# Column sums of an 8192 x 8192 float32 matrix: three pieces of TensorE work moved within the tail of a load-bound kernel

## The chip, the cores and the metric

The kernel runs on one core of one Trainium2 chip. The time is the device time of one execution in microseconds (us). A run of a kernel gives several executions, each with its span (first to last instruction) and the mean granted TensorE clock; one execution, the first of a run, also leaves a profile (the profile of the kernel before is of an execution of 627.52 us, apart from the three in its table).

## The reference

```python
def setup_inputs():
    return {"x": np.random.randn(8192, 8192).astype(np.float32)}

def reference(x):
    return np.sum(x, axis=0)
```

The sum runs over rows. On the chip rows lie on partitions, so most of the sum is elementwise addition of row blocks by VectorE, and the last step, over the 128 partitions, is a matmul with a matrix of ones.

## The kernel before

The 8192 rows come as 32 loads of 256 rows (128 partitions x 2 rows x 8192 columns, 8 MB each) into three buffers. VectorE adds 31 of them into a running row. The last load is cut so that little work is left when its last byte has come: its first row of each partition comes in two halves of 4096 columns, its second row in six strips.

```python
STRIPS = [2048, 2048, 2048, 1024, 768, 256]
...
for h in range(2):                       # first row, two halves
    i = nc.sync.dma_start(out=rows(last, 0, c0, w), in_=xl[0][:, c0 : c0 + w])
    ...
    i.then_inc(s_half[h], 16)
for n, w in enumerate(STRIPS):           # second row, six strips
    nc.sync.dma_start(
        out=rows(last, 1, c0, w), in_=xl[1][:, c0 : c0 + w]
    ).then_inc(s_strip[n], 16)
```

For each strip n (0 to 5; "the third strip" is strip 2, "the sixth" strip 5) TensorE adds up three pieces in PSUM, the memory that it writes its sums to: **half n**, the first row's columns; **carry n**, VectorE's running row; **strip n**, the second row's columns. A piece is four matmuls on four column tiles, each recorded as two passes with a weight load apiece: 8 matmul records and 8 weight loads, 16 instructions. There are 18 pieces, 288 instructions.

```python
def half(n, sem=None):
    piece_sums(rows(last, 0), n, True, sem, 16)
def carry_sums(n):
    piece_sums(rows(near, 1), n, False, s_dve, carry[min(n, 3)])
def strip_sums(n):
    piece_sums(rows(last, 1), n, False, s_strip[n], 16).then_inc(s_pe, 1)

half(0, s_half[0]); half(1); carry_sums(0); carry_sums(1)   # one line each in the kernel
half(2, s_half[1]); strip_sums(0); strip_sums(1)
carry_sums(2)
for n in (3, 4, 5):
    half(n)
strip_sums(2); carry_sums(3); strip_sums(3)
carry_sums(4); carry_sums(5); strip_sums(4); strip_sums(5)
```

After each strip's sum, ScalarE or VectorE copies it out of PSUM, and three small stores end the program.

## Time and profile before

| | before |
|---|---|
| median of its first three executions | 627.25 us (627.19 to 627.32) |
| span of the profiled one | 625.6 us |
| bytes read | 268.44 MB, at 429 GB/s over the span |
| VectorE busy | 85% |
| TensorE busy | 2%, all after 607.5 us |
| second strip lands | 617.22 us |
| last TensorE pass | 622.51 us |

How to read it: the loads fill the span and the engines follow them. What TensorE does matters only from where it stops waiting for data. The prediction below shows the lines.

### The profile page before, as it was taken

Reading aid. Unit: us, or ns where it says so; the run is one execution under the profiler, and the core shown is the slowest. Engines: PE = TensorE matmul, PEld = TensorE weight load, DVE = VectorE, ACT = ScalarE, POOL = GpSimd, SP = SyncE. Lnnn points to the kernel's source line nnn. Section 1 sums busy time; section 2 is a strip of 40 time slices with the busy share of each in tenths; the row PEclk is TensorE's granted clock in tenths of the full one; section 3 lists DMA queues with packets and bytes.
Section 4 is the critical chain, followed back from the end, with each engine's and each line's share of the span. In section 5 each row is a group of like instructions: output and inputs, shape, how many; then the busy total and the mean of one; then the engine's idle time right before and its main releaser. Section 6 shows DMA issues by size and latency. Waiting matters only on the chain. (4 is left out here: it accounts for less than half of the span.)

```text
span 625.6 us, 571 instructions
## 1 busy us (share of the span) xinstructions
PE 13.2 (2%) x144; PEld 4.1 (1%) x144; DVE 531.2 (85%) x66; ACT 3.4 (1%) x5; POOL 0.3 (0%) x5
## 2 busy tenths in 40 slices
PE   0000000000000000000000000000000000000016
PEld 0000000000000000000000000000000000000002
DVE  0538988889888899888898888988889888899887
ACT  0000000000000000000000000000000000000001
POOL 0000000000000000000000000000000000000000
PEclk9999999999999999999999999999999999999999
DMA  9999999999999999999999999999999999999997
GB/s 402 402 469 402 465 406 465 406 465 406 448 423 432 440 419 453 402 469 402 469 402 469 402 469 402 465 406 465 406 465 406 453 419 432 440 423 448 402 435 306
DMA packets 5661, 268.49 MB, mean 429 GB/s; under 512 B 652, under 2 KB 784, under 8 KB 1052
## 3 DMA queue, kind: packets, MB, share of 16 engines
q1 hardware_dynamic: 5660, 268.47, 99.2%
q8 instruction: 1, 0.02, 0.0%
HBM read 268.44 MB, written 0.03 MB: 429 GB/s over the span
## 5 line engine op out<-in xcount | busy, mean ns | idle before, releaser
L121 DVE TENSOR_TENSOR buf<-buf,buf 128x8192 f32<-128x8192 f32 x29 | 252.1, 8693 | 58.1 <-DVEq L116 58.1
L126 DVE TENSOR_TENSOR buf<-buf 128x8192 f32<-128x8192 f32 x29 | 252.1, 8693 | 6.9 <-DVEq L116 6.9
L132 DVE TENSOR_TENSOR buf<-buf 128x8192 f32<-128x8192 f32 x1 | 8.7, 8691 | 23.1 <-DVEq L116 23.1
L94 PE MATMUL ps<-buf,ones 128*32 128x512 f32 (+3 forms) x144 | 13.2, 513 | 609.5 <-DMA buf<-in_x_dram 609.1
L81 DVE TENSOR_TENSOR buf<-buf,buf 128x4096 f32<-128x4096 f32 x2 | 8.8, 4422 | 1.6 <-DMA buf<-in_x_dram 1.6
L81 DVE TENSOR_TENSOR buf<-buf 128x2048 f32<-128x2048 f32 (+1 forms) x3 | 8.9, 3000 | 0.1
L94 PEld LDWEIGHTS ps<-buf,ones 128*32 128x32 f32 x144 | 4.1, 117 | 618.5 <-DMA buf<-in_x_dram 610.9
L217 ACT COPY res<-ps 128x512 f32<-128x512 f32 (+1 forms) x4 | 2.1, 520 | 618.7 <-PE ps L94 618.7
L217 DVE COPY res<-ps 128x256 f32<-128x256 f32 (+1 forms) x2 | 0.7, 325 | 2.0 <-PE ps L94 2.0
L217 ACT ACT_TABLE_LOAD x1 | 1.3, 1283 | 1.0 <-DVEq L106 1.0
L107 POOL MEMSET ones<- 128x32 f32 x1 | 0.1, 126 | 0.6 <-DVEq L106 0.6
L262 POOL MEMSET const-bfloat16-1.0<- 128x1 bf16 x1 | 0.1, 102 | 0.0
L262 POOL MEMSET const-uint8-127<- 128x1 uint8 x1 | 0.1, 102 | 0.0
L262 POOL MEMSET const-float32-0.0<- 128x1 f32 x1 | 0.1, 99 | 0.2 <-issue 0.2
L262 POOL MEMSET const-float32-1.0<- 128x1 f32 x1 | 0.1, 99 | 0.0
## 6 DMA issues: line engine op xcount, KB each, us to landing
buf<-in_x_dram SPq DMA_DIRECT2D x2, 2048.0 KB, 17.5
buf<-in_x_dram SPq DMA_DIRECT2D x3, 1024.0 KB, 23.6
buf<-in_x_dram SPq DMA_DIRECT2D x1, 512.0 KB, 26.4
buf<-in_x_dram SPq DMA_DIRECT2D x31, 29.7
buf<-in_x_dram SPq DMA_DIRECT2D x1, 384.0 KB, 26.8
buf<-in_x_dram SPq DMA_DIRECT2D x1, 128.0 KB, 26.7
out_dram<-res SPq DMA_DIRECT2D x2, 4.0 KB
out_dram<-res SPq DMA_DIRECT2D x1, 24.0 KB
```

What stands on the lines that cost most here:

```text
L81: i = nc.vector.tensor_tensor(out=o, in0=a, in1=b, op=ADD)
L94: i = nc.tensor.matmul(out=ps[n][32 * j : 32 * j + 32, 0 : w // NJ], lhsT=ones[:], rhs=runs[:, j], start=start, stop=True, skip_group_chec ...
L107: nc.gpsimd.memset(ones[:], 1.0).then_inc(s_one, 1)
L121: nc.vector.tensor_tensor(out=r0, in0=r0, in1=bufs[(b - 1) % NBUF][:, 1, :], op=ADD).then_inc(s_op, 1)
L126: nc.vector.tensor_tensor(out=r1, in0=r1, in1=r0, op=ADD).then_inc(s_buf[(b + 1) % NBUF], 1)
L132: nc.vector.tensor_tensor(out=rows(0, 1), in0=rows(0, 1), in1=rows(0, 0), op=ADD).then_inc(s_buf[1], 1)
L217: c = nc.vector.tensor_copy(out=o, in_=p) if n in (3, 5) else nc.scalar.copy(o, p)
L262: nc = _bacc.Bacc("TRN2", target_bir_lowering=False, num_devices=1)
```

## The change

The intent is to use a gap. TensorE stands idle for 1.39 us ahead of the second strip, while halves 3, 4 and 5, whose data is there, are done later, when TensorE is pressed. The change puts half 3 into that gap, halves 4 and 5 behind the second strip, and carry 2, which waits for VectorE's third piece, just ahead of the third strip.

```diff
         strip_sums(0)
+        half(3)
         strip_sums(1)
+        half(4)
+        half(5)
         carry_sums(2)
-        for n in (3, 4, 5):
-            half(n)
         strip_sums(2)
```

No load, no addition and no buffer is touched.

## The prediction

> **What bounds the kernel now.** The page comes first: the whole program is a stream of DMA loads, and TensorE works only at its very end.
>
> ```profile
> PE 13.2 (2%) x144; PEld 4.1 (1%) x144; DVE 531.2 (85%) x66; ACT 3.4 (1%) x5; POOL 0.3 (0%) x5
> ...
> HBM read 268.44 MB, written 0.03 MB: 429 GB/s over the span
> ```
>
> 268.44 MB in 625.6 us is the bound, with the one DMA queue at 99.2% of its 16 engines. The change does not touch a load, a VectorE addition or a buffer release; it moves eight-matmul pieces within TensorE's program. So only the tail after the last VectorE release of a buffer can move, and I read that next: the chain that ended last, in order of time (start, us, what).
>
> ```profile
> 593.61 23.61 DMA buf<-in_x_dram
> 617.22 0.04 issue
> 617.26 5.53 PE ps L94 x96
> 622.80 0.02 issue
> 622.82 0.22 DVE res L217
> ```
>
> The second strip lands at 593.61 + 23.61 = 617.22 us, then TensorE runs 96 matmuls until 622.8, and the last copy follows. 96 is twelve pieces of 8 (four column tiles, each as two float32 passes): strip 1, carry 2, halves 3, 4 and 5, strip 2, carry 3, strip 3, carries 4 and 5, strips 4 and 5. Taken alone the chain says "TensorE is the end", and a piece taken out is gained in full. Whether that holds depends on when the later strips land, which the chain does not show. So I went through the timeline in short windows. First TensorE around the second strip, with its weight loads:
>
> ```profile
> 614.81 1.06 PE L94 MATMUL ps<-buf,ones 128*32 128x512 f32 x8 [0.20 <-DMA buf<-in_x_dram]
> 617.26 0.64 PE L94 MATMUL ps<-buf,ones 128*32 128x512 f32 x4 [1.39 <-DMA buf<-in_x_dram]
> 618.22 0.13 PEld L94 LDWEIGHTS ps<-buf,ones 128*32 128x32 f32 x4 [0.80 <-DVE buf L81]
> 619.11 0.13 PEld L94 LDWEIGHTS ps<-buf,ones 128*32 128x32 f32 x4 [0.30 <-issue]
> 619.97 1.04 PE L94 MATMUL ps<-buf,ones 128*32 128x512 f32 x8
> 622.51 0.24 PE L94 MATMUL ps<-buf,ones 128*32 128x64 f32 x4
> ```
>
> TensorE is idle for 1.39 us before the second strip. Carry 2 starts at 618.22, when VectorE's third piece is there; half 3 starts at 619.11, strip 2 at 619.97 with no wait noted, and the last pass at 622.51. From 618.22 on it runs without a gap.
>
> Then the landings, for the issues of the third strip and of the last three (start of the issue from the timeline, time to landing from the list of DMA issues):
>
> ```profile
> 594.08 0.43 SPq L178 DMA_DIRECT2D buf<-in_x_dram  x1
> buf<-in_x_dram SPq DMA_DIRECT2D x1, 1024.0 KB, 25.6
> ...
> 595.03 0.43 SPq L178 DMA_DIRECT2D buf<-in_x_dram  x1
> buf<-in_x_dram SPq DMA_DIRECT2D x1, 512.0 KB, 26.4
> buf<-in_x_dram SPq DMA_DIRECT2D x1, 384.0 KB, 26.8
> buf<-in_x_dram SPq DMA_DIRECT2D x1, 128.0 KB, 26.7
> ```
>
> The six strip issues are 0.475 us apart (593.13, 593.61, 594.08, 594.56, 595.03, 595.51). Strip 2 therefore lands at 594.08 + 25.6 = 619.7, strip 3 at 594.56 + 26.4 = 621.0, strip 4 at 595.03 + 26.8 = 621.8 and strip 5 at 595.51 + 26.7 = 622.2, each to about 0.05 because the view rounds to tenths. Strip 2's matmuls at 619.97 are thus only some 0.25 us later than its data. That is the point of this case.
>
> **What the Trainium skill says.** "TensorE: Matmul & The Clock Gate", Part 3, says matmuls start and end strictly in program order and column tiles run concurrently. The trace agrees: four 512-column matmuls share one 0.43 us pass (start to start), so a piece moved in the program moves on the engine by just that. Its Part 1 says an idle window of about 3.4 us halves the array's clock. The first two halves do show 0.85 us per pass in place of 0.43 us, but the idle time to be filled is 1.39 us and the passes after it are already fast, so I count nothing for warmth. "PSUM — Partial Sum Buffer", the four PSUM rules, warns that two open accumulation groups in one bank and quadrant clear each other's bits; here each strip has its own 2 KiB tile, so the new interleaving is safe. "DMA: Bandwidth & Descriptors", section Where 436 GB/s comes from, puts the load ceiling at 435.2 GB/s; 429 measured over the span agrees, and nothing is to be had there.
>
> **The change part by part.** Durations are start-to-start spacings of the passes in the timeline: 512 columns 0.43 us, 256 columns 0.215, 192 columns 0.16, 64 columns 0.055, each piece being two passes.
>
> 1. Half 3 (2 x 0.215 = 0.43 us) moves into the idle 1.39 us. Strip 0's second pass starts at 615.26, so half 3 runs from about 615.69 to 616.12 plus a 0.2 us tail, done 0.9 us before strip 1 lands. It costs nothing there and leaves the chain after 617.26: minus 0.43 us.
> 2. Halves 4 and 5 (2 x 0.16 + 2 x 0.055 = 0.43 us) move from behind carry 2 to ahead of it. They take no work away, but cover the wait for VectorE. Strip 1's second pass starts at 617.72, so without a wait the next pass could start at 618.15; it starts at 618.22. Gain 0.07 us. With halves 4 and 5 there, carry 2 starts at 618.15 + 0.43 = 618.58, well after VectorE's third piece.
> 3. Together strip 2 would be ready to start at 618.58 + 0.86 = 619.44, against 619.97 before: 0.53 us earlier. But its data lands at 619.73 and the wait passes 0.04 us later, as with strip 1 (617.22, 617.26). So it starts at 619.77; and after a wait the first pass takes 0.46 rather than 0.43 us (617.26 to 617.72), which costs 0.03. Gain left: 619.97 - 619.77 - 0.03 = **0.17 to 0.18 us**. The other 0.33 us becomes a wait for the DMA.
> 4. From there the order is as before, all of it about 0.18 us earlier: carry 3 at 620.65 (its VectorE piece ends at 618.09 + 2.29 = 620.38: no wait), strip 3 at 621.08 (landed 621.0), carries 4 and 5 from 621.51, strip 4 at 621.95 (landed 621.83), strip 5 at 622.27 (landed 622.2), the last pass at 622.33 in place of 622.51. The margins at strips 4 and 5 are below 0.1 us, the rounding of the view, so up to 0.1 us could be lost there.
> 5. The copies and the last store hang on the last pass. The queue of the three stores must not become the chain: they are issued at 621.70, 622.43 and 623.12 and take 0.56 to 0.68 us each. The first hangs on strip 2's copy, which also comes 0.18 us earlier, the second on strip 3's, the third on strip 5's; all three shift alike.
>
> Sum: 627.25 - 0.18 = **627.07 us**, 0.03% less.
>
> **The rivals.** (a) Full gain: the chain shortens by all 0.50 us of parts 1 and 2, giving 626.75. For it: the chain shows 96 matmuls back to back and no DMA inside. Against it: strip 2's landing at 619.7 and strip 5's at 622.2; no order can end before 622.2 + 0.04 + two passes of 64 columns and their tail (about 0.3 us), 622.55, which is what part 4 gives already. (b) No gain: landings later than I read by the rounding, or a run with slower loads, make the wait for strip 5 take up everything: 627.2 to 627.25. The spread of the three runs, 627.19 to 627.32, is nearly as large as the gain. (c) A loss: halves 4 and 5 push carry 2 back by 0.36 us and, were strip 2's data early, strip 2 with it; that needs a strip 2 landing before 619.3, and even then half 3 out of the way leaves the end earlier. If half 3 ran slowly enough in the gap to hold up strip 1, the loss would be under 0.2 us: 627.4. It has 0.9 us to spare.
>
> **Range and chances.** My main theory has 0.18 us, (a) 0.5 us, (b) 0, (c) minus 0.2. The order within the tail can move the time by a few tenths; the rest of the range is for loads that differ a little between sessions, as 429 GB/s over 625 us leaves 0.1% = 0.6 us to small things. So 626.7 to 627.5. Two per cent is 12.5 us, more than twice the whole chain after the second strip: neither faster nor slower by that much is possible by this change.
>
> **What would show it.** Right: half 3's matmuls near 615.7 in the idle time; strip 1 still at 617.26; no VectorE wait ahead of carry 2, which starts near 618.6; a new wait for the DMA of about 0.3 us ahead of strip 2, near 619.77; a last pass near 622.33; and a chain of waits that goes through the landing of the third strip (or of a later one) in place of the second, with some 56 matmuls after it in place of 96. Wrong: strip 2 with no DMA wait and a last pass near 622.0 (rival a, my landings misread); a new wait ahead of strip 4 or 5 of over 0.1 us (rival b); landings of the strips that move although no load was touched, which would mean that the loads' own variation, not TensorE's order, decides.

## The result, and the profile after

The first six executions of the changed kernel took 627.00, 627.29, 628.82, 628.51, 627.35 and 627.58 us: median 627.47 us, mean 627.76 us. Six of the kernel before had a median of 627.29 us. The ratio is 1.0007 (95% interval 0.9994 to 1.002): the same. Ratios are the mean time of one kernel's runs over that of the other's in the same rounds, so not quite the ratio of the medians quoted. Executions over 1.5% slower than the fastest of the same kernel are left out of the means.

The profile after is of the 627.00 us execution. First its chain that ended last (start, us, what):

```profile
593.84 25.61 DMA buf<-in_x_dram
619.45 0.04 issue
619.49 2.89 PE ps L94 x56
622.38 0.02 issue
622.40 0.23 DVE res L218
```

The chain now goes through the landing of the third strip, at 619.45 us, with 56 matmuls behind it, as part 3 of the prediction had it. Then its timeline around the second strip, from short windows:

```profile
615.47 0.61 PE L94 MATMUL ps<-buf,ones 128*32 128x256 f32 x8
617.03 0.64 PE L94 MATMUL ps<-buf,ones 128*32 128x512 f32 x4 [0.95 <-DMA buf<-in_x_dram]
617.91 0.57 PEld L94 LDWEIGHTS ps<-buf,ones 128*32 128x32 f32 x20 [0.30 <-issue]
618.35 1.04 PE L94 MATMUL ps<-buf,ones 128*32 128x512 f32 x8
619.49 0.16 PEld L94 LDWEIGHTS ps<-buf,ones 128*32 128x32 f32 x8 [1.01 <-DMA buf<-in_x_dram]
```

Half 3 (256 columns) runs in the gap, which shrinks to 0.95 us. The weight loads of halves 4, 5 and carry 2 follow strip 1 without a wait for VectorE; carry 2 starts at 618.35 and the third strip waits for the DMA. Carry 2's second pass starts at 618.78, so TensorE could have gone on at 618.78 + 0.43 = 619.21; it goes on at 619.49, a wait of 0.28 us.

All strips land earlier here than in the profile before (the second at 616.99 in place of 617.22), though no load was touched. To compare two kernels' tails one therefore measures from a landing. From the records of the two traces, the last TensorE pass starts 0.314 us after the sixth strip's landing before and 0.126 us after it now, and the span ends 3.445 and 3.254 us after it. The change is worth **0.19 us** in the tail, where 0.18 was predicted. And yet the mean rose, from 627.33 to 627.76 us: the two executions at 628.5 and 628.8 us are the question.

### The profile page after: what moved, and what is told of

Read it like the earlier page. It is cut to its first block, busy times and chain, and to the rows that moved or that the text cites. A ratio compares the mean times of both kernels' runs of the same rounds, so it can differ in the third digit from the quotient of the medians.

```text
span 625.2 us, 571 instructions
## 1 busy us (share of the span) xinstructions
PE 13.2 (2%) x144; PEld 3.9 (1%) x144; DVE 531.2 (85%) x66; ACT 3.4 (1%) x5; POOL 0.3 (0%) x5
## 6 DMA issues: line engine op xcount, KB each, us to landing
buf<-in_x_dram SPq DMA_DIRECT2D x1, 128.0 KB, 26.7
```

## The experiments

Two theories stood at first. **L**: the loads vary from execution to execution, and long executions have nothing to do with TensorE. **T**: the new order makes TensorE's tail fragile. Both fell in part, and a third, **F**, came out of a lucky profile.

The table gathers the traces that the sections below use. All rows are from the records of each run's trace. "Behind" is how much later the sixteenth, last engine reports the sixth strip done than the fifteenth: a load is complete when sixteen completions are recorded.

| kernel | span | sixth strip lands | last pass after it | end after it | behind |
|---|---|---|---|---|---|
| before | 625.64 | 622.20 | 0.31 | 3.45 | 0.24 |
| before_again | 625.57 | 622.13 | 0.31 | 3.43 | 0.17 |
| before_third | 625.39 | 621.96 | 0.31 | 3.43 | 0.05 |
| changed | 625.22 | 621.97 | 0.13 | 3.25 | 0.02 |
| after_again | 625.23 | 621.96 | 0.14 | 3.27 | 0.02 |
| after_third | 625.47 | 622.21 | 0.13 | 3.26 | 0.05 |
| half3_only | 625.54 | 622.29 | 0.13 | 3.25 | 0.27 |
| none_in_gap | 625.34 | 621.99 | 0.22 | 3.35 | 0.04 |
| fill_small | 627.01 | 623.82 | 0.13 | 3.20 | 1.52 |
| fill_large | 626.49 | 621.87 | 1.50 | 4.62 | 0.01 |
| one_engine_35kb | 626.84 | 623.59 | 0.14 | 3.25 | 1.42 |
| one_engine_70kb | 629.36 | 626.12 | 0.13 | 3.24 | 3.68 |
| early_8 | 627.88 | 623.20 | 1.55 | 4.68 | 1.25 |
| early_13 | 626.21 | 622.97 | 0.13 | 3.24 | 0.97 |
| early_3 | 626.82 | 623.56 | 0.14 | 3.26 | 1.28 |
| early_1 | 626.41 | 623.15 | 0.14 | 3.26 | 1.23 |
| one_tile | 625.37 | 622.11 | 0.14 | 3.27 | 0.13 |
| half5_late | 625.51 | 622.14 | 0.25 | 3.37 | 0.06 |
| half5_late_again | 625.38 | 622.02 | 0.23 | 3.36 | 0.01 |
| before_early_1 | 627.08 | 622.03 | 1.92 | 5.05 | 0.14 |

### The two kernels again

No edit: the changed kernel and the kernel before, twice each.

> The changed kernel once more. Two of its first six executions took 628.5 and 628.8 us, the other four 627.0 to 627.6. Theory L (the loads vary from execution to execution, whatever TensorE's order): such long executions turn up here at any rate and in the kernel before as well, and the profile shows the end at a fixed distance after the landing of the sixth strip, 3.25 us in the changed kernel (3.45 us before). Theory T (the new order makes the tail fragile, for example TensorE still at half speed when the last strips come): long executions stay with the changed kernel, about one in three, and in a long one the tail after the sixth strip's landing is itself over 1 us longer.

> The kernel before against itself, as a measure of what two equal kernels differ by. Theory L: ratio within 0.2% of 1, with single executions above 628 us possible. Theory T: no execution above 628 us.

> The changed kernel a third time, as the control of this call: fetch near 621.3 to 621.8, tail 3.25 us after the sixth strip's landing, most executions 627.0 to 627.6 and about one in four at 628.4 to 629.

> The kernel before a third time: most executions 627.2 to 627.6, about one in six above 628.4; tail 3.44 us. The median of the fast majority of the changed kernel should lie 0.1 to 0.25 us below this one's.

Measured: after_again 627.00, 627.06, 628.48, 627.22, 627.33 (ratio 1.0003); after_third 627.34, 627.32, 627.34, 628.52, 627.01, 628.81 (ratio 0.9999). The kernel before against itself: before_again 627.49, 627.28, **629.03**, 627.48, 627.25 (ratio 1.0007, as large as the change's own); before_third 627.17, 627.48, 627.45, 627.83, **629.05**, 627.43 (ratio 1.0000).

So the kernel before has long executions too. With the executions of it beside the others (the six beside the first result, none of them long, are left out, as no clock is listed for them), 10 of 67 of its executions lie at 628.85 to 629.26 us, the other 57 at 627.12 to 627.83 (mean 627.39). Of the changed kernel's 17 executions 5 lie at 628.48 to 628.82 and 12 at 627.00 to 627.58 (mean 627.24). The short ones differ by 0.15 us, near the 0.19 us of the traces; over all executions the means are 627.63 and 627.65. **In these executions the gain is there and is given back in long ones.** Theory T in its plain form (only the changed kernel has them) is out.

### Which part of the change pays

half3_only:

```diff
         half(3)
         strip_sums(1)
+        carry_sums(2)
         half(4)
         half(5)
-        carry_sums(2)
         strip_sums(2)
```

> Only half 3 moves into the idle time ahead of the second strip; halves 4 and 5 stay behind carry 2. By the prediction's own steps carry 2 still waits for VectorE's third piece, and the third strip is then ready about 0.10 us after its data: nothing of what halves 4 and 5 cover is worth anything. Expected: the third strip still waits for its landing (by some 0.2 us in place of 0.3), last pass and end at the same distance after the sixth strip's landing as in the changed kernel (3.25 us). Rival: moving halves 4 and 5 is worth the 0.07 us of the VectorE wait, so 3.32 us.

none_in_gap:

```diff
-        half(3)
         strip_sums(1)
+        half(3)
         half(4)
         half(5)
```

> Halves 3, 4 and 5 all behind the second strip and ahead of carry 2, none in the idle time before it. TensorE then reaches the third strip some 0.07 to 0.1 us earlier than before, later than its landing, so with no wait for it: the end 3.35 us after the sixth strip's landing, between 3.45 (before) and 3.25 (changed). If the idle time ahead of the second strip were not what pays, it would equal the changed kernel's 3.25.

Measured: 3.25 us after the sixth landing with half 3 alone, 3.35 us with none in the gap, both as expected. Half 3 in the gap alone gives the whole 0.19 us. Halves 4 and 5 ahead of carry 2 give 0.1 us by themselves and nothing on top of it: with half 3 gone, what they cover is swallowed by the wait for the third strip. Times: half3_only 627.32, 628.55, 627.33, 628.66, 627.39; none_in_gap 627.12, 627.13, 627.18, 627.41, 627.39. The intervals of both ratios (1.0010 and 0.9999, each about 0.0014 either way) hold 1.

### Is the wait ahead of the third strip real?

Useless matmuls into a spare PSUM tile between carry 2 and strip 2: fill_small has one set of four of 128 columns, fill_large two of 512.

```diff
         carry_sums(2)
+        for _ in range(2):                     # fill_small: 1
+            for j in range(NJ):
+                nc.tensor.matmul(
+                    out=spare[32 * j : 32 * j + 32, 0:512],     # fill_small: 128
+                    lhsT=ones[:], rhs=rows(last, 0, 512 * j, 512),
+                    start=True, stop=True, skip_group_check=True,
+                )
         strip_sums(2)
```

> The changed kernel with useless matmuls into a spare PSUM tile, between carry 2 and the third strip: four column tiles of 128 columns, two passes of 0.107 us, 0.21 us in all, in a wait for the third strip that the profile of the changed kernel puts at 0.28 us. If that wait is real, nothing moves: the tail after the sixth strip's landing stays at 3.25 us, the last pass 0.13 us after that landing. If TensorE still set the end: 3.46 us.

> The same with two pieces of 512 columns, 4 passes of 0.43 us = 1.72 us. The 0.28 us wait and the later strips' small margins swallow 0.35 us of it: the last pass comes 1.37 us later than in the changed kernel, tail 4.6 us, time about 628.6. TensorE's order thus costs its full size once the waits are filled.

Measured: in fill_small's profile the third strip, landed at 619.82, is still waited for after the useless matmuls:

```profile
619.87 0.16 PEld L96 LDWEIGHTS ps<-buf,ones 128*32 128x32 f32 x8 [0.19 <-DMA buf<-in_x_dram]
```

TensorE goes on 0.05 us after the landing, as in the changed kernel (0.04): 0.21 us of matmuls for nothing, so the wait is real. (The 0.13 us after the sixth landing says nothing here, as that landing was itself late, see below.) fill_large comes to 4.62 us after the landing, 628.27 to 628.60 us, as worked out: of its 1.72 us the waits take 0.35 and no more.

fill_small's other executions took 627.30 to 627.33 us, but the profiled one 628.79. Its chain that ended last:

```profile
595.12 0.43 SPq L180
595.55 0.04 issue
595.59 28.23 DMA buf<-in_x_dram
623.82 0.04 issue
623.86 0.36 PE ps L96 x8
```

The first five strips landed as always (the fifth at 621.97). The sixth, 128 KB, took 28.23 us in place of 26.7, and TensorE stood waiting for its last eight matmuls. In the records of the trace fifteen of the strip's sixteen completions are in at 622.29, the last at 623.82. The only other traffic of that time is one instruction fetch of 16 KB, listed on the page as its own queue (q8):

```
fill_small, trace records (us)     fetch 621.80 to 622.73 (0.931)
completion writes (4 bytes, 9 ns each)  ... 621.75 621.82 622.00   622.72 (25 ns)   then only stores, from 623.26
sixth strip, completions           621.88 ... 622.11 622.29   623.82
```

One completion write is recorded exactly when the fetch ends, and that strip is complete 1.1 us after it. The records name no engine for a packet; that fetch and late completion share one is inferred from these times, and why the strip is 1.52 us late behind a fetch of 0.93 us stays open. This is **theory F**: an engine's own program is fetched by DMA too, and in a long execution the fetch stands in front of the last strip's completion on one DMA engine.

### What does a delay of one engine cost?

An extra load of 17 rows ahead of load 15, into a tile of its own:

```diff
+            if t == 15:
+                nc.sync.dma_start(out=extra[:], in_=x[0:17, 0:512]).then_inc(
+                    s_extra, 16                        # one_engine_70kb: 0:1024
+                )
...
+        nc.sync.wait_ge(s_extra, 16)
         store(nc.sync, 0, 2, s_act, 3)
```

> The changed kernel with one extra load of 17 rows of 2 KB (34.8 KB, 0.013% of the bytes) in mid-stream, ahead of load 15. Seventeen rows do not divide over the engines, so it should fall to one DMA engine alone. In the traces so far a 64 KB packet takes 2.418 us on one engine, so 34.8 KB is about 1.28 us of one engine's time. Theory L, in its exact form (every landing waits for the slowest of 16 engines, and an engine that fell behind never catches up, as the traces show one engine 0.02 to 0.33 us behind from the first load to the last): the end moves by the whole 1.3 us, to 628.5 us, which is the size of the long executions; the tail after the sixth strip's landing stays 3.25 us. Rival (the loads share the bytes, so one engine's delay is absorbed in the queue of the others): +0.08 us, that is 627.3.

> The same with rows of 4 KB (69.6 KB, 0.026% of the bytes). Theory L: twice the delay, +2.6 us, 629.8 us, tail still 3.25 us. Rival (absorbed): +0.16 us, 627.4.

Measured: medians 628.36 and 631.01 us. The 17 packets of 2 KB took 1.42 us in sum, and one engine was 1.42 us behind at the end; the 17 of 4 KB took 3.82 us (0.16 to 0.33 us each, more than the 0.16 reckoned), and one engine was 3.68 us behind. That miss of size aside, the delay is kept from the middle of the stream to the last strip (1.19 us at load 15, 1.41 at load 21, 1.42 at the sixth strip; 3.56 and 3.68 with the larger load): 0.013% of the bytes cost 0.17% of the time. **An engine that is this far behind does not catch up, and the end waits for the slowest.** Small lags, of 0.01 to 0.33 us after the first load, mostly stay too (half5_late's shrinks from 0.13 to 0.03 and grows again), which fits the small spread of the short executions.

### Whose fetch is it?

Useless small pieces (32 columns) ahead of half 0, while TensorE has nothing to do: D = 8 and 13, later 3 and 1.

```diff
         nc.tensor.wait_ge(s_one, 1)
+        for _ in range(D):
+            for j in range(NJ):
+                nc.tensor.matmul(
+                    out=spare[32 * j : 32 * j + 32, 0:32],
+                    lhsT=ones[:], rhs=ones[:],
+                    start=True, stop=True, skip_group_check=True,
+                )
         half(0, s_half[0])
```

> The changed kernel with eight small useless pieces (32 columns, 128 instructions) ahead of half 0, while TensorE has nothing to do. In one profile that fell on a long execution the sixth strip's landing came 1.5 us late on one DMA engine, and just before it the one instruction fetch of the tail (16 KB, 0.93 us, begun 621.80) ended, at 622.73. Theory F: that fetch is TensorE's own next block of program, asked for about where its eleventh piece is issued, and a long execution is one in which it goes in front of the last strip's completion on its engine. With eight more pieces ahead it is asked for near the third real piece, about 611 to 613 us: the record of the fetch moves there, ahead of the end of the loads, no execution lies above 628.3 us because of the last strip, and one engine may instead fall behind by up to 0.9 us (the fetch's own time), so 627.2 to 628.1 us. Rival: the fetch belongs to another engine or to the time of day; it stays near 621.5 and about one execution in four stays long.

> Thirteen such pieces (208 instructions): by theory F the first fetch comes within some microseconds of the start of the program, while the first loads fill, and costs at most 0.9 us there; a second block[...] is asked for sixteen pieces later, at the fourteenth real piece, about 620 to 621 us, so a fetch near the end is there again and long executions with it. Rival: one fetch near 621.5 as before, whatever the number of pieces.

Measured: the fetch of 16 KB is at 614.91 us with D = 8, and at 7.58 us with D = 13, where the list of DMA queues shows two:

```profile
q8 instruction: 2, 0.03, 0.0%
```

It moves with TensorE's instruction count, so it is TensorE's program. In early_13 one engine is 1.16 us behind at the first load, 0.93 to 1.01 from the seventh on, and all five executions lie at 627.96 to 628.13 us. Its second fetch came at 622.86, later than expected, and made no execution long: that part of the expectation was wrong. In early_8 the fetch came later than the 611 to 613 us expected and held one engine up by 1.33 us at the second strip, not 0.9: the executions took 627.97 to 629.65 us, four of five above the range expected.

early_8's profile, of the 629.65 us execution, has a second surprise: the end comes 4.68 us after the sixth landing. The late second strip made TensorE's gap 2.28 us, and behind it the passes of 192 columns are 0.32 us apart, not 0.16. TensorE ran at half speed, and the mean clock of that execution is 0.997. This is theory T's mechanism after all; it comes back below.

### Is the fetch what makes long executions?

one_tile asks for the fetch later by taking 48 instructions out ahead of the strips. Its result is wrong on purpose (relative error 0.59); its TensorE is as long at work.

```diff
-        for j in range(NJ):
+        for j in range(tiles):      # 1 for halves and carries 0 and 1, else NJ
             i = nc.tensor.matmul(
 ...
-                start=start,
+                start=start or (n < 2 and j > 0),
```

> Wrong result on purpose (columns 0 to 4095 lack three quarters of two parts): halves and carries 0 and 1 run one column tile in place of four, so TensorE is as long at work but has 48 instructions fewer ahead of the strips. Theory F: the fetch is asked for about three pieces later, near the fourteenth piece (strip 3, 621.0 us in place of 618.35), is recorded after 621.6, mostly when all engines have finished the sixth strip, and no execution is long: all within 626.9 to 627.6 us. If long executions have another cause: one in four at 628.4 to 629.

> Three useless pieces (48 instructions) ahead of half 0. Theory F: the fetch is asked for three pieces earlier, at the second strip (617.03 us), and comes while the engines still have strips to move, around 619.5 to 621: it then holds up one engine by about 0.9 us in nearly every execution: most executions between 627.8 and 629.0, few or none at 627.0 to 627.4. Rival: as the changed kernel.

> One useless piece (16 instructions) ahead of half 0: the fetch is asked for at half 5, some 0.1 us earlier than in the changed kernel. Theory F expects a small change: long executions in a quarter to a half of the runs, the others at 627.0 to 627.4.

Measured:

| kernel | instructions ahead | fetch recorded | executions, us |
|---|---|---|---|
| one_tile | -48 | 621.87 | 627.15 627.40 627.13 627.16 627.12 |
| changed (three profiles) | 0 | 621.27, 621.43, 621.72 | 12 of 17 short, 5 long |
| early_1 | +16 | 620.51 | 628.19 628.30 628.47 628.65 628.28 |
| early_3 | +48 | 620.80 | 628.60 628.77 628.38 628.74 628.65 |

All of ten are long with the fetch earlier, and none of five with it later (at 5 in 17 that alone has a chance of 18%; with the ten of half5_late below, 0.5%). The ratios of early_3 and early_1 to the kernel before, 1.0016 and 1.0013, are still "same" by the 2% rule, and only the first interval (from 1.0003) leaves 1 out. early_1 was expected to do it in a quarter to a half, and did it in all; the order of early_1 and early_3 in the record also shows that I cannot say to the microsecond when a fetch is served. The chain of early_1, whose second line is the landing of the fifth strip on an engine that the fetch held up by 1.25 us:

```profile
594.72 0.04 issue
594.76 28.08 DMA buf<-in_x_dram
622.84 0.04 issue
622.88 0.69 PE ps L96 x16
```

The changed kernel stands at the edge: one piece of 16 instructions more, and every execution is long. From the counts I put the request near TensorE's eleventh piece, an estimate; one_engine_70kb fits it, where TensorE stood between its eleventh piece (622.51) and the late third strip (623.58) and the fetch is recorded at 623.13. The eleventh piece is half 5 at 619.86 us in the profile before and carry 2 at 618.35 after. By this count **the change, in moving work forward, moves its own program fetch forward**, into the last strips.

The count is not proved. The records, nearly all of short executions, do not show the change's fetch earlier: the kernel before has it at 621.46 to 621.54, within the changed kernel's 621.27 to 621.72. And two kernels do not fit it: in half3_only the eleventh piece is half 5 at 619.52 us, much later than the changed kernel's 618.35, yet two of five are long (clock 0.999); in none_in_gap it is carry 2 at 618.81, and none of five is long.

### And the long executions of the kernel before?

The kernel before asks for the fetch later, but has long executions too. Its edit: the same useless piece, D = 1, in the kernel before.

> The kernel before with one useless piece (16 instructions) ahead of half 0. Its eleventh piece is then half 4 at 619.54 us in place of half 5 at 619.86, still 1.2 us later than in the changed kernel. If only the moment of the request counts, its share of long executions stays near that of the kernel before (8 of 55), at most like the changed kernel's. If an extra piece matters in another way (for example by moving where in the program the block ends relative to a wait), all executions are long as with early_1.

Measured: 628.86, 627.42, 627.58, 627.41, 628.87. An extra piece by itself does not make every execution long. The profiled execution was a long one again, and it is of another kind. Its sixth strip landed in time (622.03), but the last pass came 1.92 us later. The busy time by stage (stretch and length, then PE, PEld, DVE, ACT, POOL, then the granted clock, DMA share and GB/s), of before_early_1 and then of the profile before:

```profile
615.00:617.00 2.00, 0.71 (x8) 0.00 (x0) 1.97 (x2) 0.58 (x1) 0.00 (x0) 1.00 1.01 426
617.00:619.00 2.00, 1.90 (x12) 0.52 (x16) 2.00 (x2) 0.09 (x1) 0.00 (x0) 0.58 0.98 412
619.00:621.00 2.00, 2.00 (x20) 0.60 (x16) 1.19 (x1) 0.49 (x1) 0.00 (x0) 0.56 1.00 407
```

```profile
617.00:619.00 2.00, 1.74 (x16) 0.45 (x20) 2.00 (x2) 0.59 (x1) 0.00 (x0) 1.00 0.96 406
619.00:621.00 2.00, 2.00 (x40) 1.02 (x36) 1.37 (x1) 0.00 (x0) 0.00 (x0) 1.00 1.03 416
```

The granted clock averages 0.58 and 0.56 in the two stretches behind the gap (in the trace's clock records it is 0.5 from 617.34 to 620.75 us), and TensorE did 20 matmuls in the second, where it otherwise does 40. Its timeline there:

```profile
617.10 0.91 PE L96 MATMUL ps<-buf,ones 128*32 128x512 f32 x4 [1.39 <-DMA buf<-in_x_dram]
617.76 1.10 PE L96 MATMUL ps<-buf,ones 128*32 128x512 f32 x4
618.62 1.10 PE L96 MATMUL ps<-buf,ones 128*32 128x512 f32 x4
619.47 1.10 PE L96 MATMUL ps<-buf,ones 128*32 128x512 f32 x4
```

Passes 0.86 us apart in place of 0.43, after an idle gap of 1.39 us, the very gap that the change fills.

The clock that each execution lists tells the two kinds apart. All 10 long executions of the kernel before, and both of before_early_1, have a mean clock of 0.997; every short one of the kernel before has 0.999 or 1.0. The 5 long ones of the changed kernel have 1.0, 0.999, 0.999, 0.999 and 0.998. A slow stretch as in before_early_1 costs 3.41 us x 0.5 / 627 us = 0.0027 of the mean, which is 0.997. A long execution at 0.998 or 0.999 is another thing: in early_1's profile (0.998) the clock falls at 624.34 us, when TensorE has done its last pass. No execution of the kernel before is long at such a clock, so loads that are late by this much of themselves did not occur in its 67. So the kernel before loses by half speed and the changed kernel by the fetch. For the changed kernel this is inferred from the clock and from its neighbours' traces; no long execution of itself was profiled.

### A version free of both?

half5_late keeps half 3 in the gap and asks for the fetch later, by making strip 2 the eleventh piece:

```diff
         half(4)
-        half(5)
         carry_sums(2)
         strip_sums(2)
+        half(5)
```

> The changed kernel with half 5 (64 columns, 0.11 us) behind the third strip, so that the eleventh piece is strip 2 at 619.5 us in place of carry 2 at 618.35. Theory F: long executions become rarer than in the changed kernel (5 of 17 there), at best none; the 0.11 us now lies behind the third strip's landing, so the tail is 3.36 us in place of 3.25, and the typical execution 627.1 to 627.4 us.

> The changed kernel with half 5 behind the third strip, a second time. If it is free of both kinds of long execution: five more executions between 627.1 and 627.5 us at a clock of 1.0, so none of ten long, where the changed kernel's share of 5 in 17 would leave that a chance of about 3%. If it only makes them rarer: one or two above 628.3.

Measured: 627.29, 627.34, 627.23, 627.23, 627.34, and 627.16, 627.54, 627.16, 627.61, 627.32: none of ten long, the clock 1.0 in all, the fetch at 621.66. The chain that ended last in half5_late:

```profile
594.02 25.64 DMA buf<-in_x_dram
619.67 0.04 issue
619.71 2.96 PE ps L94 x64
```

Eight matmuls more lie behind the third strip than in the changed kernel, and the end comes 3.37 us after the sixth landing, as expected. The mean of ten is 627.32 us, 0.3 us below both other kernels' means. It is the best of the correct ones by its mean, but not proved so: at the 10 in 67 of the kernel before, ten executions without a long one have a chance of about 0.85^10 = 20%, at the changed kernel's 5 in 17 about 3%. Against the kernel before in the same rounds its ratios are 0.9995 and 0.9997, with intervals that hold 1.

## Why the prediction was right or wrong

- **What bounds the kernel; parts 1 to 5, as far as TensorE's own order goes**: right. Half 3 in the gap, carry 2 without its VectorE wait, a wait for the third strip of 0.28 us (0.33 predicted), 56 matmuls after that landing, the last pass 0.19 us earlier against the sixth landing (0.18 predicted). half3_only, none_in_gap and fill_small confirm it one by one.
- **Rival (a), the full gain**, is refuted by the wait for the third strip. **Rival (b), no gain**, fails in the tails of the short executions. In long ones its mechanism came about, by a cause that it did not name: a wait for a late strip near the end (1.05 us ahead of the fifth in early_1, 1.30 ahead of the sixth in fill_small). The prediction's own sign of being wrong, landings that move although no load was touched, came true with it. **Rival (c)** in its own terms did not occur: no piece held up a strip.
- **"It costs nothing there"** (part 1) is the step that failed. It counted what the moved pieces cost TensorE, not that TensorE's program is itself a load on the DMA engines, 16 KB of it asked for at a point in the instruction order. Nothing in the chain or the groups shows it, but the page does: its list of DMA queues has one instruction packet. I did not ask when it comes. In place of 0.18 us less in every execution, 5 of 17 were long, at 628.48 to 628.82 us, against 627.24 for the short ones, and the mean did not fall. early_1 and early_3 show that an earlier fetch makes executions 1.1 to 1.4 us longer; that it is the fetch in the changed kernel's own long executions is inferred, and why this order brings it on rests on the count above.
- **"So I count nothing for warmth"** failed too, but in the other direction: it hid a gain, so it is not why the time came out above the prediction. The prediction saw a gap of 1.39 us, read that the clock halves after 3.4 us, and took the one profile with fast passes as the rule. In 10 of 67 executions of the kernel before the clock was down, and before_early_1 shows it down behind that gap. None of the 17 changed executions shows the 0.997, nor any of the other 53 of kernels with half 3 in the gap (early_8, with its gap of 2.28 us, apart), against 12 of 77 of the kernels that leave it open.
- **The range**, 626.7 to 627.5, rested on the spread of three executions and on 0.6 us for loads that differ between sessions. It holds the median of 627.47, but neither the mean of 627.76 nor three of the six executions. What it took for a small continuous spread has two heights: short executions, and long ones 1.2 to 1.9 us up. The reason given, loads that vary, fits the spread of the short ones (one engine behind by 0.01 to 0.33 us).
- **No change beyond 2%** was right.

Open are: why the clock drops in one execution and not in the next; which instruction exactly asks for the fetch, and why half3_only has long executions; whether 5 in 17 and 10 in 67 truly differ as shares. On the first the clock records give a hint that no run tests: in before_early_1 and early_8 the clock rose at 610.51 and 612.37 us and fell 6.83 us later in both, within 0.9 us of the end of the gap, for 3.41 us; in the 17 other profiles with such records it stayed up for 13.65 us. Of the five profiles with the gap of 1.39 us, the one that fell had the earliest rise. So it may be where the gap lies after the rise that decides, and not its length alone.

## What to carry to other kernels

In a kernel that is bound by its loads, a moved instruction saves only what lies between the end of its wait and the next landing; work that out from landings, not from the chain of waits. An engine's delay of a microsecond in mid-stream was still there at the end here, and the fetch of a program can be such a delay, so when instructions are moved or added, look where the instruction fetch comes. And before a few tenths of a microsecond are believed, run the kernel before against itself: here two equal kernels differed by as much as the change.

## What the Trainium skill lacked or had wrong

- "Runtime: NRT & Kernel Launch", Instruction fetch mechanics, says that program comes in 16 KiB blocks by a DMA queue of the sequencer's own (the traces agree: one packet of 16384 bytes, moved by TensorE's instruction count), and that crossing a block costs a tail-bump, "mostly hidden". In this load-bound kernel it is not hidden from the loads: a fetch of 0.93 us, one engine still 0.97 to 1.25 us behind at the sixth strip (early_13, early_1, early_8), and 1.52 us where it stands ahead of the last completion (fill_small).
- "TensorE: Matmul & The Clock Gate", Part 1, asks for an idle window of about 3.4 us before the clock halves. Here the clock was down after gaps of 1.39 us (before_early_1; by the 0.997 also 10 of 67 executions of the kernel before) and 2.28 us (early_8), and in before_early_1 stayed down for 3.41 us (passes some 0.86 us apart from 617.76 to 620.32, 0.43 after that). None of the 17 executions of the changed kernel, with a gap of 0.95 us, shows it.
- No page that I found says that a DMA engine which falls behind in a stream of loads stays behind: one that was 1.41 us behind at load 21 was 1.42 us behind at the last strip (one_engine_35kb).
